# Score products over pairs of chunks, keys turned without a stride, and value products per pair of kv heads in a hybrid decoder step

## The chip, the cores and the metric

The kernel runs on one core of one Trainium2 chip as one launch. The metric is the device time of that launch in microseconds (us), as the median of several runs. A profiled execution of the same program gives the rows used below: for each engine what ran when, and what ended its waits. The engines are TensorE (PE, and PEld for its weight loads), VectorE (DVE), ScalarE (ACT), GpSimd (POOL) and SyncE (SP), which issues most of the transfers.

## The reference, cut to what matters

The program is one step of a two-layer decoder: 512 prompt tokens and, for each of 8 requests, 8 new tokens behind 2048 cached ones. Layer 0 mixes by pooling, layer 1 is sparse attention; each is followed by a gated FFN. The change touches only the attention of the new tokens in layer 1. There each of 16 heads (4 query heads for each of 4 kv heads, 64 wide) attends in three branches: to compressed rows, to 16 selected blocks of 64 rows, and to a window of 512 rows. The three results are weighed by gates and added.

```python
N_HEADS = 16
KV_HEADS = 4
HEAD_DIM = D_MODEL // N_HEADS
Q_PER_KV = N_HEADS // KV_HEADS
SEL_BLOCK = 64
N_SEL = 16
WINDOW = 512

def masked_softmax(s, mask):
    s = jnp.where(mask, s.astype(jnp.float32), NEG)
    return jnp.where(mask, jax.nn.softmax(s, axis=-1), 0.0)
```

All of it is float32. The selected branch is computed over all 2048 cached rows, with a bias of -1e30 on the rows of blocks that aren't selected.

## The kernel before

`sample_attention` (L1055) holds the attention of the new tokens. For each request `b` there are five **chunks** `ch`: chunk 0 is the window of 512 rows, chunks 1 to 4 are 512 rows each of the selected-branch cache. That makes 40 steps, `i = 5b + ch`. The 32 query rows of a kv head's group (4 heads by 8 tokens) and the 4 kv heads fill 128 partitions in the scores.

- `load(i)` (L1179) brings a raw tile of 512 rows, four rows to a partition (row `4p + j`), keys in the first 256 columns of each row and values in the other 256. The window comes by SP's DMA (L1189), and its rows go out again to an output (L1191); the other four chunks come by a gather that POOL issues (L814). There are 12 raw slots; the values of a chunk free its slot.
- `prepare(i)` (L1197) turns the keys on DVE by 32 by 32 squares (L1205) into `kf`, of which there are two buffers. The transpose writes every fourth word, so that the keys stand in the cache's own order (`n j`).
- `score(i)` (L1217) makes 32 products (2 halves of the head's 64 columns, 4 row groups `q`, 4 kv heads `g`), each on a 32 by 32 tile of PE, of 128 columns (L1236), into one of four places of a ring in PSUM. DVE adds the bias, takes the maximum and writes `sc` (L1244). `softmax` follows after chunk 0 and after chunk 4 (L1251, ACT's exponentials L1260, L1261).
- `turn` (L1266) brings a chunk's weights into rows by four transposes on PE (tile `ppt`, L202) and a copy on ACT (`ph`, L1275).
- `values` (L1279) multiplies them with the chunk's values: 4 rows `j` by 4 kv heads, 16 products of 64 columns on tiles of 128 rows by 32 columns (L1294), into `po`. Its sixth call for a request takes the compressed rows (`cvb`) and the new tokens (`VT`). `outputs` (L1297) and `outputs2` (L1309) add the branches and turn the result.

A float32 product is two records on PE, and two weight loads on PEld. At step `i` the loop (L1317) calls `load(i+5)`, `prepare(i+1)`, `score(i)`, and `turn` and `values` of the request before. A scheduler orders each engine's queue by what each instruction needs, so that the program's order is a wish and not a rule. Ahead of the loop stands the compression of cached rows for all 8 requests (`rounds` L942, with DVE's transposes `xf` at L882, the splits `xlo` at L886, the hidden rows `hs`, `hgh`, `hgl` at L932 to L939, and the compressed values `cvf`, which go by DMA to `cvd`, L988 to L990). The first keys of the attention are turned during its last rounds. Other places that rows name are `select` (L1153) and `select2` (L1171), which choose blocks, `qq` (L1094), the queries by 32 by 32 squares, and L1430, a product of the prompt's attention.

Of the kernel before, what the change touches and what calls it, by code (L numbers as in the profile page):

```python
# [9 lines left out]
F32 = mybir.dt.float32  # L10
# [11 lines left out]
NB = 8  # L22
# [33 lines left out]
PT = 4  # L56
SR = 5
WORD = (0, 1, 2, 3, 4)

# [69 lines left out]
def body(tc, top, I, O):  # L129
# [925 lines left out]
    def sample_attention(ctx):  # L1055
# [4 lines left out]

        VT = sa.tile([128, 4, 2, 64], F32, name="VT")

# [13 lines left out]
        with ExitStack() as c1:  # L1076
# [6 lines left out]
            for j in range(2):  # L1083
                c0 = KC + 512 * (j + 1) + 256
                sp.dma_start(VT[64 * j:64 * j + 64, :, j], pjd[:, c0:c0 + 256].rearrange("t (g c) -> t g c", g=4))

# [27 lines left out]

        kp_ = Slots(ctx, "sk", kf=2)
        more = Slots(ctx, "sv")
# [78 lines left out]
        kv, prepared = {}, set()  # L1195

        def prepare(i):  # L1197
            if i >= len(steps) or i in prepared:
                return
            b, ch = steps[i]  # L1200
            prepared.add(i)
            raw = raws.pop(i)

            kf = kp_.tile([128, 2, 4, 128], F32, tag="kf", name=f"kf{b}{ch}")
            dve.transpose(kf.rearrange("p f g (n j) -> p j g f n", j=4), raw[:, :, 0:256].rearrange("p j (g f i) -> p j g f i", g=4, f=2))  # L1205
            kv[b, ch] = (kf, raw)

        def attend(between):
# [6 lines left out]
            ring = mmt("pss", "s", 4)  # L1215

            def score(i):  # L1217
                b, ch = steps[i]
                kf, _ = kv[b, ch]
                if i % 5 == 0:  # L1220
# [10 lines left out]
                pt = ring[:, :, (i % 4) * 128:(i % 4 + 1) * 128]  # L1231
                for f in range(2):
                    for q in range(4):
                        for g in range(4):
                            qs = slice(32 * q, 32 * q + 32)
                            pe.matmul(pt[32 * g:32 * g + 32, q], qq[qs, b, g, f], kf[qs, f, g], start=f == 0, stop=f == 1,  # L1236
                                      tile_position=(32 * q, 32 * g))
                by_key = "p (q n j) -> p q n j"
# [40 lines left out]
            def values(b, ch):  # L1279
                ph = pend.pop((b, ch))  # L1280
                cvb = st[b][4]
                if ch == 0:
                    po[b] = mmt(f"po{b}")
                raw = kv.pop((b, ch))[1] if ch < 5 else None
                for j in range(4 if ch < 5 else 2):
                    for g in range(4):
                        if ch < 5:
                            v, c0 = raw[:, j, 256 + 64 * g:320 + 64 * g], 64 if ch == 0 else 0
                        elif j == 0:
                            v, c0 = cvb[:, 64 * g:64 * g + 64], 128  # L1290
                        else:
                            v, c0 = VT[:, g].rearrange("q s c -> q (s c)"), 0
                        rs = slice(32 * g, 32 * g + 32)
                        pe.matmul(po[b][rs, c0:c0 + v.shape[1]], ph[:, j, rs], v,  # L1294
                                  start=ch == 0 and j == 0, stop=ch == 5 and j == 1, tile_position=(0, 32 * g))

            def outputs(b):  # L1297
                osb = scp.tile([128, 3, 64], F32, tag="osb", name=f"osb{b}")
                mx = st[b][2]
                tmp = osb[:, 2]  # L1300
                act.activation(tmp, po[b][:, 128:192], AF.Copy)
                dve.scalar_tensor_tensor(tmp, po[b][:, 64:128], mx[:, 15:16], tmp, OP.mult, OP.add)

                twice = [128, 2, 64]
                dve.scalar_tensor_tensor(osb[:, 0:2], po[b][:, 0:64].unsqueeze(1).broadcast_to(twice), mx[:, 11:12],
                                         tmp.unsqueeze(1).broadcast_to(twice), OP.mult, OP.add)
                return osb[:, 0:2].rearrange("p s c -> p (s c)")

# [7 lines left out]

            prepare(0)  # L1317
            for i in range(len(steps) + 7):
                b, ch = divmod(i, 5)
                between(i)  # L1320
                load(i + SR)
                prepare(i + 1)
                if b < NB:
                    score(i)
                    if ch == 3:
                        turn(b, 0)
                if 0 < b <= NB:
                    if ch >= 1:
                        turn(b - 1, ch)
                    if ch == 4:  # L1330
                        turn(b - 1, 5)
                    if ch >= 2:
                        values(b - 1, ch - 1)
                if b < NB and ch == 4:
                    values(b, 0)
                if b > 1:
                    if ch == 0:
                        values(b - 2, 4)
                        values(b - 2, 5)
                        pend["o"] = outputs(b - 2)  # L1340
                    elif ch == 1:
                        outputs2(b - 2, pend.pop("o"))
# [466 lines left out]
```

## Time and profile before

| quantity | value |
|---|---|
| median of 3 runs | 1721.8 us (1721.6 to 1725.24) |
| the profiled execution: time | 1727.31 us |
| its span in the trace | 1725.5 us |
| PE, PEld busy in the span | 1625.2 us, 1504.4 us |
| DVE, ACT, POOL busy | 1044.1, 758.7, 405.0 us |
| new tokens' scores, first to last product | 854.3 to 1022.8 us of the span |
| bytes moved by DMA | 206.35 MB |

The profiled execution took 5.5 us more than the median, and 1.8 us of its time lie around the span. The page cuts the span in 40 slices and gives for each the busy share of the engines in tenths. Of these slices, numbers 21 to 24 (863 to 1035 us) show PE at 7 to 8 tenths, DVE at 5 to 7, and the clock granted to PE at 6 to 7 tenths. In most other slices PE stands at 9. The rows behind these words, and those of the waits, follow in a section of their own.

### The profile page before, as it was taken

The numbers are of one execution on the slowest core, as the hardware profiler recorded it, in microseconds if no ns is written. First come the engines' busy times: TensorE is split into PE (matmuls) and PEld (weight loads), VectorE is DVE, ScalarE is ACT, GpSimd is POOL, SyncE is SP. The second block draws the span as 40 slices with busy tenths as digits, with TensorE's granted clock in tenths as the row PEclk, the third lists the DMA queues.
The fourth block names the chain that finished last, engine by engine and source line by source line (L and its number), as shares of the span: only waits on it lengthen the run. The fifth ranks groups of instructions, "written<-read, shape, count | busy, mean of one in ns | idle before, by whom it ended". The sixth has DMA issues, their size and how long they took to land.

```text
span 1725.5 us, 36745 instructions
## 1 busy us (share of the span) xinstructions
PE 1625.2 (94%) x15447; PEld 1504.4 (87%) x15447; DVE 1044.1 (61%) x2029; ACT 758.7 (44%) x1384; POOL 405.0 (23%) x602
## 2 busy tenths in 40 slices
PE   8999999999999999999877788999999999999995
PEld 7999999999999999999754454555999999999995
DVE  7666454545574448888775556767366555464547
ACT  5654334343353325566533235656155535344331
POOL 2222111111020023433311204665022112011104
PEclk9999999999999999999967778999999999999998
DMA  5232232223257746645657771001412232222311
GB/s 188 82 99 99 66 106 75 80 68 98 63 183 244 191 149 217 227 150 183 226 200 275 241 218 43 1 1 45 135 50 74 74 98 74 74 98 74 98 59 55
DMA packets 123461, 206.35 MB, mean 120 GB/s; under 512 B 19039, under 2 KB 98745, under 8 KB 112832
## 3 DMA queue, kind: packets, MB, share of 16 engines
q1 hardware_dynamic: 113392, 134.49, 24.7%
q0 software_dynamic: 9216, 67.11, 11.4%
q8 instruction: 121, 1.98, 0.5%
q10 hardware_dynamic: 688, 2.40, 0.4%
q14 instruction: 44, 0.36, 0.1%
HBM read 178.85 MB, written 24.84 MB: 118 GB/s over the span
## 4 chain that ended last, share of the span: by engine, by line
PE 79%; issue 7%; DVE 7%; POOL 4%; ACT 3%; DMA 1%; SPq 0%; ACTq 0%; POOLq 0%; DVEq 0%
PE u L165 31%; PE d L165 14%; PE pr L911 10%; PE pj L165 7%; PE pss L1236 3%; PE wo L165 2%; POOL P L1505 2%; PE ppt L202 2%; PE psp L1486 1%; PE po L1294 1%; PE pop L1534 1%; PE pj L709 1%; DVE kf L1205 1%; DVE wla L257 1%; DVE lnst L320 1%
## 5 line engine op out<-in xcount | busy, mean ns | idle before, releaser
L165 PE MATMUL u<-xl,wha 128*128 128x288 f32 x704 | 208.0, 296 | 0.3 <-POOL xl L351 0.2
L165 PE MATMUL u<-xl,whb 128*128 128x288 f32 x704 | 208.0, 296 | 0.2
L165 PE MATMUL u<-xh,whb 128*128 128x288 f32 x704 | 207.3, 295 | 0.0
L165 PE MATMUL u<-xh,wha 128*128 128x288 f32 x704 | 207.3, 295 | 0.0
L165 PE MATMUL u<-xh,wla 128*128 128x288 f32 x704 | 207.2, 295 | 0.0
L165 PE MATMUL u<-xh,wlb 128*128 128x288 f32 x704 | 207.2, 295 | 0.0
L417 POOL COPY fcol<-u 128x18 f32<-128x18 f32 x88 | 68.0, 782 | 467.8 <-ACT u L416 467.8
L422 DVE SCALAR_TENSOR_TENSOR c<-u,convp,c 128x592 f32<-128x592 f32 x88 | 72.3, 832 | 123.1 <-ACT c L421 123.1
L257 DVE TENSOR_TENSOR wla<-rawa,wha 128x2048 fp32r<-128x2048 f32 (+1 forms) x52 | 99.5, 1918 | 68.6 <-ACT wha L256 67.9
L257 DVE TENSOR_TENSOR wlb<-rawb,whb 128x2048 fp32r<-128x2048 f32 x37 | 84.8, 2293 | 86.4 <-ACT whb L256 86.4
L165 PEld LDWEIGHTS u<-xl,wha 128*128 128x128 f32 x704 | 132.0, 188 | 2.0 <-DVE xl L351 1.1
L165 PEld LDWEIGHTS u<-xl,whb 128*128 128x128 f32 x704 | 132.0, 188 | 1.9 <-DVE xl L351 1.1
L165 PEld LDWEIGHTS u<-xh,wha 128*128 128x128 f32 x704 | 132.0, 188 | 0.1
L165 PEld LDWEIGHTS u<-xh,whb 128*128 128x128 f32 x704 | 132.0, 188 | 0.1
L165 PEld LDWEIGHTS u<-xh,wlb 128*128 128x128 f32 x704 | 132.0, 188 | 0.0
L165 PEld LDWEIGHTS u<-xh,wla 128*128 128x128 f32 x704 | 132.0, 188 | 0.0
L503 DVE SCALAR_TENSOR_TENSOR xz<-xz,d 128x288 f32<-128x288 f32 x160 | 70.4, 451 | 87.7 <-PE d L165 87.2
L256 ACT ACTIVATE wha<-rawa 128x2048 fp32r<-128x2048 f32 (+1 forms) x52 | 83.1, 1617 | 91.1 <-PE d L165 58.9
L256 ACT ACTIVATE whb<-rawb 128x2048 fp32r<-128x2048 f32 x37 | 70.9, 1915 | 114.3 <-PE d L165 32.0
L911 PE MATMUL pr<-xlo,W1h 128*128 128x256 f32 x512 | 104.6, 286 | 2.7 <-DVE xlo L886 2.7
L911 PE MATMUL pr<-xhi,W1h 128*128 128x256 f32 x512 | 105.6, 288 | 0.0
L165 PE MATMUL d<-hh,wha 128*128 128x288 f32 x352 | 104.4, 298 | 0.1
(654 smaller groups left out, 4614.6 us busy)
## 6 DMA issues: line engine op xcount, KB each, us to landing
rawa<-in_ffn_w_up SPq DMA_DIRECT2D x22, 1024.0 KB
rawb<-in_ffn_w_up SPq DMA_DIRECT2D x22, 1024.0 KB
rawa<-in_ffn_w_down SPq DMA_DIRECT2D x11, 1024.0 KB
rawb<-in_ffn_w_down SPq DMA_DIRECT2D x11, 1024.0 KB
rawa<-in_nsa_w_in SPq DMA_DIRECT2D x9, 1024.0 KB
sr<-in_state_win_kv SPq DMA_DIRECT2D x8, 1024.0 KB
out_win_kv_s<-sr SPq DMA_DIRECT2D x8, 1008.0 KB
rawb<-in_nsa_w_o SPq DMA_DIRECT2D x16, 256.0 KB
```

The source lines that it names most:

```text
L165: pe.matmul(out, a, b, start=first and j == 0, stop=last and j == n - 1)
L202: pe.transpose(out, in_, ident[:in_.shape[0], :in_.shape[0]])
L256: act.activation(h[:, a:b], r[:, a:b], AF.Copy)
L257: dve.tensor_tensor(lo[:, a:b], r[:, a:b], f32(h[:, a:b]), OP.subtract)
L320: dve.bn_stats(self.st[:, t, q], pt[:LT])
L417: pool.tensor_copy(col[:, :, m].rearrange("p (j i) -> p j i", i=2), u[:, TP:TP + 90].rearrange("p (j i) -> p j i", i=10)[:, :, 0:2])
L422: dve.scalar_tensor_tensor(c, u[:, 1:1 + CW], cv[:, 44 + m:45 + m], c, OP.mult, OP.add)
L503: dve.scalar_tensor_tensor(z, z, ALPHA if first else 1.0, p_[:, :HALF], OP.mult, OP.add)
L709: pe.matmul(*args, start=k == 0 and i == 0, stop=k == KD - 1 and i == 1)
L911: pe.matmul(banks[b, kv][ri][:, :, gh * nn:(gh + 1) * nn], W1[wi][:, kv, ri * 8 + th * 4 + c], xx[:, c // 2, c % 2].rearrange("p g n -> p ...
L1236: pe.matmul(pt[32 * g:32 * g + 32, q], qq[qs, b, g, f], kf[qs, f, g], start=f == 0, stop=f == 1, tile_position=(32 * q, 32 * g))
L1505: pool.tensor_tensor(x, x, st[:, 2, e, t:t + 1].broadcast_to([128, (t + 1) * 128]), OP.mult)
```

## The change

Three things change, all of them in `sample_attention`.

1. **Scores by groups of chunks.** The five chunks of a request form three groups: chunk 0 alone, 1 with 2, 3 with 4. A group has one `kf`, and `products` makes its 32 products at once, of 128 columns or, for a pair, of 256. DVE's transpose now writes its words side by side, so the keys stand in the order `j n`. The order of the cache is restored where PE writes into PSUM: there each product's words are written four words apart (a view `s j n` of a place laid out as `s n j`). There are three `kf` buffers, each of up to two chunks, where there were two of one chunk.
2. **Keys earlier.** Three chunks are prepared ahead of the loop, and step `i` prepares `i + 3`, where it was one and `i + 1`.
3. **Values by pairs of kv heads.** Each value product takes the weights of two kv heads (a tile of 128 rows by 64 columns) and the values of both, 128 columns; half of what it computes, one head's weights with the other's values, is not used. A chunk has 8 products of 128 columns instead of 16 of 64. `VT`, `po` and `outputs` follow: `po` has 384 columns where 192 were, and `outputs` takes a copy of 128 columns on ACT and two steps of 128 columns on DVE.

The records of the products fall from 2560 to 1536 for the scores, and from 1408 to 704 for the values; each record has its weight load.

```diff
-        VT = sa.tile([128, 4, 2, 64], F32, name="VT")
+        VT = sa.tile([128, 2, 2, 128], F32, name="VT")
...
-        kp_ = Slots(ctx, "sk", kf=2)
+        kp_ = Slots(ctx, "sk", kf=KB_)
...
+        groups = [g for b in range(NB) for g in ([5 * b], [5 * b + 1, 5 * b + 2], [5 * b + 3, 5 * b + 4])]
+        group_of = {i: n for n, g in enumerate(groups) for i in g}
...
-            kf = kp_.tile([128, 2, 4, 128], F32, tag="kf", name=f"kf{b}{ch}")
-            dve.transpose(kf.rearrange("p f g (n j) -> p j g f n", j=4), raw[:, :, 0:256].rearrange("p j (g f i) -> p j g f i", g=4, f=2))
-            kv[b, ch] = (kf, raw)
+            n = group_of[i]
+            g = groups[n]
+            if i == g[0]:
+                kv["k", n] = kp_.tile([128, 2, 4, len(g), 128], F32, tag="kf", name=f"kf{n}")
+
+            at = order_of(g).index(i)
+            dve.transpose(kv["k", n][:, :, :, at].rearrange("p f g (j n) -> p j g f n", j=4),
+                          raw[:, :, 0:256].rearrange("p j (g f i) -> p j g f i", g=4, f=2))
+            kv[b, ch] = raw
+
+        def order_of(g):
+            return sorted(g, key=lambda i: i % 4)
...
+            def products(n):
+                g = order_of(groups[n])
+                b = steps[g[0]][0]
+                kf = kv.pop(("k", n))
+                places = ring.rearrange("p q (s n j) -> p q s j n", s=4, j=4)[:, :, g[0] % 4:g[-1] % 4 + 1:max(1, g[-1] % 4 - g[0] % 4)]
+                for f in range(2):
+                    for q in range(4):
+                        for h in range(4):
+                            qs = slice(32 * q, 32 * q + 32)
+                            pe.matmul(places[32 * h:32 * h + 32, q], qq[qs, b, h, f], kf[qs, f, h].rearrange("p s (j n) -> p s j n", j=4),
+                                      start=f == 0, stop=f == 1, tile_position=(32 * q, 32 * h))
+
             def score(i):
                 b, ch = steps[i]
-                kf, _ = kv[b, ch]
+                if i == groups[group_of[i]][0]:
+                    products(group_of[i])
...
-                for f in range(2):
-                    for q in range(4):
-                        for g in range(4):
-                            qs = slice(32 * q, 32 * q + 32)
-                            pe.matmul(pt[32 * g:32 * g + 32, q], qq[qs, b, g, f], kf[qs, f, g], start=f == 0, stop=f == 1,
-                                      tile_position=(32 * q, 32 * g))
...
-                    for g in range(4):
+                    for p in range(2):
                         if ch < 5:
-                            v, c0 = raw[:, j, 256 + 64 * g:320 + 64 * g], 64 if ch == 0 else 0
+                            v, c0 = raw[:, j, 256 + 128 * p:384 + 128 * p], 128 if ch == 0 else 0
...
-                        rs = slice(32 * g, 32 * g + 32)
-                        pe.matmul(po[b][rs, c0:c0 + v.shape[1]], ph[:, j, rs], v,
-                                  start=ch == 0 and j == 0, stop=ch == 5 and j == 1, tile_position=(0, 32 * g))
+                        pe.matmul(po[b][64 * p:64 * p + 64, c0:c0 + v.shape[1]], ph[:, j, 64 * p:64 * p + 64], v,
+                                  start=ch == 0 and j == 0, stop=ch == 5 and j == 1)
...
-            prepare(0)
+            for i in range(3):
+                prepare(i)
...
-                prepare(i + 1)
+                prepare(i + 3)
```

The lines of the kernel after have other numbers: the scores' products are L1239 there (L1236 before), the transposes of the keys L1214 (L1205), `sc` L1264 (L1244), the value products L1313 (L1294), and a line of the compression is one higher.

Two places show how the order of the work moves. The first is DVE at the end of the compression. Before, one chunk's transpose (`kf`) stands there ahead of the last rounds; the names `xf`, `xlo`, `hs` and `hgl` are the compression's.

```order
L1205 STREAM_TRANSPOSE kf_10192<-sr_9924 128x4x4x2x32
L886 TENSOR_TENSOR xlo_9976<-xf_9974,xhi_9975 128x1024
L882 STREAM_TRANSPOSE xf_10074<-crp 128x2x4x2x32
L1134 TENSOR_REDUCE cm_9967<-psc_9964 128x1
L1135 TENSOR_TENSOR stl<-psc_9964,cst 128x16
L882 STREAM_TRANSPOSE xf_10093<-crp 128x2x4x2x32
...
L932 TENSOR_TENSOR hs_10111<-pr_9838,hs_10111 128x4x127
L886 TENSOR_TENSOR xlo_10095<-xf_10093,xhi_10094 128x512
L939 TENSOR_TENSOR hgl_10116<-hs_10111,hgh_10115 128x512
```

The same place of DVE's queue after:

```order
L1214 STREAM_TRANSPOSE kf_10195<-sr_9927 128x4x4x2x32
L1214 STREAM_TRANSPOSE kf_10195<-sr_9929 128x4x4x2x32
L887 TENSOR_TENSOR xlo_9979<-xf_9977,xhi_9978 128x1024
L1135 TENSOR_REDUCE cm_9970<-psc_9967 128x1
L1136 TENSOR_TENSOR stl<-psc_9967,cst 128x16
L883 STREAM_TRANSPOSE xf_10077<-crp 128x2x4x2x32
L1214 STREAM_TRANSPOSE kf_10303<-sr_9931 128x4x4x2x32
L883 STREAM_TRANSPOSE xf_10096<-crp 128x2x4x2x32
...
L887 TENSOR_TENSOR xlo_10098<-xf_10096,xhi_10097 128x512
L1214 STREAM_TRANSPOSE kf_10303<-sr_9933 128x4x4x2x32
L940 TENSOR_TENSOR hgl_10119<-hs_10114,hgh_10118 128x512
```

The transposes of chunks 2, 3 and 4, which stood among the attention's own steps, now stand among the last rounds of the compression, that of chunk 4 just ahead of the last `hgl`.

The second place is PE's queue in the middle of the attention, from a request's last value products on. Before:

```order
L1294 MATMUL po_11890<-VT,ph_12217 32x128 x4
L1236 MATMUL pss<-kf_12255,qq 32x128 x32
L202 MATMUL ppt_12370<-cst,sc_11912 128x128 x4
L202 MATMUL pot_12377<-cst,osb_12329 128x128
L202 MATMUL ppt_12418<-cst,sc_11912 128x128 x3
L1236 MATMUL pss<-kf_12335,qq 32x128 x32
L202 MATMUL ppt_12418<-cst,sc_11912 128x128
L1294 MATMUL po_12235<-sr_11643,ph_12375 32x64 x16
L202 MATMUL ppt_12478<-cst,sc_12257 128x128
L1236 MATMUL pss<-kf_12383,qq 32x128 x32
```

And after, from such a place on:

```order
L1313 MATMUL po_11402<-VT,ph_11627 64x256 x2
L1239 MATMUL pss<-kf_11549,qq 32x2x4x32 x32
L203 MATMUL ppt_11751<-cst,sc_11448 128x128 x4
L203 MATMUL pot_11758<-cst,osb_11711 128x128
L203 MATMUL ppt_11767<-cst,sc_11448 128x128 x4
L1313 MATMUL po_11637<-sr_11245,ph_11756 64x128 x8
L1239 MATMUL pss<-kf_11649,qq 32x2x4x32 x32
L203 MATMUL ppt_11819<-cst,sc_11683 128x128 x4
```

A pair's 32 products stand where two groups of 32 stood, and 8 value products where 16 stood; the turns (`ppt`) between them are the same. On DVE two evictions (`sc`) follow each other and then two transposes, three or four chunks ahead.

## Rows read from the trace of the kernel before

**Rows 1.** Busy time of engines by stretch: the attention's start and middle.

```profile
core 0: us, PE busy (x) PEld busy (x) DVE busy (x) ACT busy (x) POOL busy (x), PEclk, DMA share, GB/s
854.00:884.00 30.00, 23.66 (x766) 16.88 (x766) 26.29 (x56) 10.16 (x20) 3.57 (x5) 0.69 0.40 140
884.00:1010.00 126.00, 92.96 (x2779) 64.81 (x2783) 78.15 (x149) 38.92 (x87) 22.99 (x31) 0.74 0.75 265
```

**Rows 2.** Who waited for whom, 884 to 1010 us: total us, times, longest.

```profile
DVE sc L1244 <- PE pss L1236: 31.4, 20, 3.1
PE pss L1236 <- issue: 25.1, 17, 3.5
...
PE po L1294 <- issue: 2.0, 2, 1.6
```

**Rows 3.** Chain that ended last, 854 to 884, then 884 to 1010 us.

```profile
by line: DVE kf L1205 26.6%; PE pss L1236 25.9%; DVE sc L1244 14.4%; issue 9.3%; PE po L1294 5.3%; PE ppt L202 3.1%; ACT sc L1260 2.7%; DVE blk L1153 2.2%; PE psb L1171 1.9%; DVE hidp L932 1.0%; ACT ptl L1261 1.0%; DVE mx L1263 0.8%; DVE bl
...
by line: PE pss L1236 31.8%; issue 25.3%; PE ppt L202 18.4%; PE po L1294 17.4%; DVE kf L1205 3.2%; DVE sc L1244 1.5%; ACT ptl L1261 0.7%; PE pot L202 0.7%; ACT sc L1260 0.5%; DVE mx L1262 0.4%; DVE mx L1244 0.1%; DVE mx L1263 0.1%; DVE mx L
```

**Rows 4.** DMA, 884 to 1010 us: packets, MB, share; median us to landing.

```profile
DMA packets 5183, 33.41 MB, mean 265 GB/s; under 512 B 567, under 2 KB 1207, under 8 KB 1207
...
q8 instruction: 22, 0.36, 1.1%
...
sr<-in_cache_slc_kv,idx POOLq DMA_INDIRECT x20, 8.5
```

**Rows 5.** The page: PE's instructions and its instruction queue, whole span.

```profile
PE 1625.2 (94%) x15447; PEld 1504.4 (87%) x15447; DVE 1044.1 (61%) x2029; ACT 758.7 (44%) x1384; POOL 405.0 (23%) x602
...
q8 instruction: 121, 1.98, 0.5%
```

**Rows 6.** All score products: ns min/median/max, first and last start, form.

```profile
L1236 PE MATMUL pss<-kf,qq x2560: 264/412/419, 854.3 to 1022.8; 32*32 32x128 f32 x197
```

**Rows 7.** Timeline of PE: one chunk's products, one chunk's values, twice.

```profile
864.15 1.52 PE L1236 MATMUL pss<-kf,qq 32*32 32x128 f32 x64 [1.58 <-DVE mx L1244]
865.61 1.08 PE L1294 MATMUL po<-sr,ph 128*32 128x64 f32 x32
...
876.44 1.07 PE L1236 MATMUL pss<-kf,qq 32*32 32x128 f32 x64 [0.50 <-DVE mx L1244]
877.43 0.65 PE L1294 MATMUL po<-sr,ph 128*32 128x64 f32 x32
```

**Rows 8.** Stretches as in rows 1: the granted clock at those moments.

```profile
863.00:866.60 3.60, 2.45 (x96) 1.79 (x96) 3.57 (x10) 0.21 (x1) 0.00 (x0) 0.50 0.02 5
876.40:878.00 1.60, 1.56 (x96) 1.20 (x96) 1.60 (x2) 0.17 (x1) 0.00 (x0) 1.00 0.04 10
```

**Rows 9.** Products of 512 columns on four tiles; eight in the chain.

```profile
L1430 PE MATMUL pk<-Q,KB x32: 592/617/1063, 1044.1 to 1148.6; 128*32 128x512 f32 x32
...
1107.07 1.00 PE pk L1430 x8
```

**Rows 10.** VectorE's transposes: chunk keys, compressed rows, queries.

```profile
L1205 DVE STREAM_TRANSPOSE kf<-sr x40: 1985/2036/2141, 821.2 to 1017.2; 128x1024 f32<-128x1024 f32 x40
...
L882 DVE STREAM_TRANSPOSE xf<-cr x128: 661/696/712, 597.1 to 826.6; 128x512 f32<-128x512 f32 x128
...
L1094 DVE STREAM_TRANSPOSE qq<-q x1: 2268/2268/2268, 682.5 to 682.5; 128x2048 f32<-128x2048 f32 x1
```

**Rows 11.** Timeline ahead of the attention: two gathers, one VectorE piece.

```profile
826.95 0.95 POOL L814 DMA_INDIRECT sr<-in_cache_slc_kv,idx  x1 [4.55 <-DVE xf L882]
...
839.19 1.47 POOL L814 DMA_INDIRECT sr<-in_cache_slc_kv,idx  x1 [3.64 <-DVE xf L882]
...
844.16 1.43 DVE L939 TENSOR_TENSOR hgl<-hs,hgh 128x512 fp32r<-128x512 f32 x1 [1.15 <-ACT hgh L938]
```

**Rows 12.** Chain into the attention's first product.

```profile
847.95 4.39 DMA cvd<-cvf
...
854.27 1.54 PE pss L1236 x63
```

More of the change, by code (lines that the diff above doesn't have):

```diff
@@ L57 @@
 SR = 5
+KB_ = 3
 WORD = (0, 1, 2, 3, 4)
@@ L1084, in sample_attention @@
                 c0 = KC + 512 * (j + 1) + 256
-                sp.dma_start(VT[64 * j:64 * j + 64, :, j], pjd[:, c0:c0 + 256].rearrange("t (g c) -> t g c", g=4))
+                sp.dma_start(VT[64 * j:64 * j + 64, :, j], pjd[:, c0:c0 + 256].rearrange("t (a c) -> t a c", a=2))
             q4 = s1.tile([128, NB, 4, 64], F32, name="q4")
@@ L1283, in values @@
                     po[b] = mmt(f"po{b}")
-                raw = kv.pop((b, ch))[1] if ch < 5 else None
+                raw = kv.pop((b, ch)) if ch < 5 else None
                 for j in range(4 if ch < 5 else 2):
-                    for g in range(4):
+                    for p in range(2):
                         if ch < 5:
-                            v, c0 = raw[:, j, 256 + 64 * g:320 + 64 * g], 64 if ch == 0 else 0
+                            v, c0 = raw[:, j, 256 + 128 * p:384 + 128 * p], 128 if ch == 0 else 0
                         elif j == 0:
-                            v, c0 = cvb[:, 64 * g:64 * g + 64], 128
+                            v, c0 = cvb[:, 128 * p:128 * p + 128], 256
                         else:
-                            v, c0 = VT[:, g].rearrange("q s c -> q (s c)"), 0
-                        rs = slice(32 * g, 32 * g + 32)
-                        pe.matmul(po[b][rs, c0:c0 + v.shape[1]], ph[:, j, rs], v,
-                                  start=ch == 0 and j == 0, stop=ch == 5 and j == 1, tile_position=(0, 32 * g))
+                            v, c0 = VT[:, p].rearrange("q s c -> q (s c)"), 0
+                        pe.matmul(po[b][64 * p:64 * p + 64, c0:c0 + v.shape[1]], ph[:, j, 64 * p:64 * p + 64], v,
+                                  start=ch == 0 and j == 0, stop=ch == 5 and j == 1)
             def outputs(b):
-                osb = scp.tile([128, 3, 64], F32, tag="osb", name=f"osb{b}")
+                osb = scp.tile([128, 128], F32, tag="osb", name=f"osb{b}")
                 mx = st[b][2]
[L1300 to L1307, printed above, removed]
+                act.activation(osb, po[b][:, 256:384], AF.Copy)
+                for j in (1, 0):
+                    dve.scalar_tensor_tensor(osb, po[b][:, 128 * j:128 * j + 128], mx[:, 11 + 4 * j:12 + 4 * j], osb, OP.mult, OP.add)
+                return osb
             def outputs2(b, osb):
```

## Prediction

> **What bounds the kernel now.** I read the busy time by stretch first, since the change lies in the new tokens' attention alone, and its stretches differ. At the start, 854 to 884 us, DVE is busy 26.29 of 30 us; in the middle, 884 to 1010 us, PE is busy 92.96 of 126 us, DVE 78.15 and the DMA engines 0.75 of the time [rows 1]. Then who waits for whom: in the middle DVE waits 31.4 us for score products, so PE is ahead of it in the chain, while PE's own idle time stands mostly at "issue", 25.1 us before scores in 17 places and 2.0 us before values in 2 [rows 2]. The chain that ended last says the same: at the start DVE's key transposes hold 26.6% of it and its evictions 14.4%; in the middle scores hold 31.8%, issue 25.3%, turns 18.4%, values 17.4%, and the key transposes 3.2% [rows 3].
>
> What is "issue"? PE waits for no engine there. In the same 126 us its instruction queue q8 moved 22 packets [rows 4]; over the whole span there are 121 for 15447 products and 15447 loads [rows 5], which is 30894/121 = 255 instructions a packet, and 22 x 255 = 5610 is about the 2779 + 2783 that PE and PEld ran there [rows 1]. I read the idle time as waiting for the instructions themselves: (25.1 + 2.0)/22 = 1.23 us a packet.
>
> **The change part by part.** The sum is made against the profiled execution's 1727.3 us, which lies 5.5 us above the median.
>
> *A, fewer instructions.* 1024 score records and 704 value records go, each with its load: 3456 instructions or 13.5 packets. At 1.23 us that is **-16.7 us**. The other bound is 0, if what delays PE is a refill that comes as often for other reasons.
> The Trainium skill ("Runtime: NRT & Kernel Launch", section "Instruction fetch mechanics") says that the sequencer fetches ahead and that crossing a block is mostly hidden. By that, A would be near 0 and the sum 16.7 us higher. The trace disagrees in this stretch, as 27.1 us of PE's idle time have no other releaser [rows 2].
>
> *B, scores.* A chunk's 64 records took 1.52 us at one moment and 1.07 at another, a chunk's 32 value records 1.08 and 0.65 [rows 7]; the granted clock was 0.50 and 1.00 then [rows 8], that is 1.2 and 2.4 GHz. The middle's mean of 0.74 [rows 1] is 48% of the time at the upper level and 52% at the lower, so a chunk's scores cost 0.48 x 1.07 + 0.52 x 1.52 = 1.30 us, a request's five 6.50. After, a request has one single group and two pairs, each of 64 records. A pair's tiles take 2 products x 2 records x 256 = 1024 columns each; as many on each of four tiles took 1.00 us at the upper level [rows 9]. The lower bound is that records, not columns, set the pace: 1.07. I add the start and end of the sixteen tiles, 1.2 at the upper level and 1.95 at the lower, mean 1.59. So 1.30 + 2 x 1.59 = 4.48, 2.0 less a request, **-16 us** for eight. The lower bound gives 6.50 - 3.90 = 2.6 a request, -21.
>
> *C, values.* Before 0.48 x 0.65 + 0.52 x 1.08 = 0.87 us a chunk. After, each of two tiles takes 4 products x 2 records x 128 = 1024 columns, 1.00 us by [rows 9], and at the lower level between 1.00 x 1.08/0.65 = 1.66 and 2.00: I take 1.75, mean 1.39. That is +0.52 for each of 40 chunks, +21. The sixth call goes from 384 columns a tile to 768, +0.37 at the upper level, +0.4 at the mix, +3 for eight. Together **+24 us**. So the change trades columns for instructions: on columns alone it would lose.
>
> *D, DVE's transposes.* With the stride 1024 columns take 2036 ns; without, 512 take 696 and 2048 take 2268 [rows 10], so 1024 should take 1.22 us: 0.82 us or 40% less. On the chain the transposes hold 0.266 x 30 + 0.032 x 126 = 12 us [rows 3]; 40% of it is -5, and some evictions come sooner behind them: **-6 us**. The bounds are 0 (PE is late next) and -12 (all of it goes).
>
> *E, the start.* Transposes of chunks 2 to 4 move ahead of the last compression rounds. The one for chunk 4 stands before the last `hgl`, which ran at 844.16; of the gathers before the attention one is issued at 826.95 and one at 839.19, 1.47 us long [rows 11], and in this kernel a gather lands 8.5 us after issue (median of the middle) [rows 4]. If chunk 4's gather is issued after the transposes that free POOL, at about 843, its landing at 851 to 852 holds `hgl`, and behind it wait `cvf`, the 4.39 us of its DMA and the first scores at 854.27 [rows 12]: +8 us. But then the keys of five chunks are ready, and the start is the stretch that DVE bounds; five transposes were 5 x 2.04 = 10 us of its 30. I take **0**, between -3 and +8.
>
> *F.* `outputs` has steps of 128 columns where it had 64 and 128, eight times, beside DVE time that waits for PE [rows 2]: 0; without that cover some 0.1 us each. The third key buffer and its size delay some early gathers; that is in E and G.
>
> *G, transposes three ahead.* DVE now asks for chunk i+3 at step i. A slot comes free some six steps before its chunk's turn; steps are (1022.8 - 854.3)/39 = 4.3 us apart [rows 6], so a gather has three steps, about 12 us, against a median of 8.5 [rows 4]. Behind a transpose that waits stand the next evictions, and PE's next group behind these. Late gathers I price at **+2.5 us**; bounds 0 and +8.
>
> Sum: -16.7 - 16 + 24 - 6 + 0 + 2.5 = -12, or 1715 us for the profiled execution and **1709 us** on the median.
>
> **The rivals.**
>
> *R1, strided writes into PSUM slow the score products (slower).* The change takes the stride from DVE and gives it to PE, which writes each product's words four apart. No row shows a product that does so. For: the same stride costs DVE a factor of 2.036/1.22 = 1.67 [rows 10]. Against: single score products are not at their column rate (512 columns a tile in 1.07 us, where 1024 take 1.00 [rows 7, 9]), so some cost hides. With 1.67 a pair's columns take 1.67 and 2.77 us, mean 2.24: 0.65 x 16 = +10, 1720 us. If the second half of the head (which adds to what stands there) reads with the stride as well, I take 2.5: pairs 3.36, +28, singles +3, so 1740 us. It decides where a pair takes more than 2.6 us on average: there the gain and 0.2% are used up.
> The Trainium skill speaks against the change here: "PSUM — Partial Sum Buffer", section "Specifications (TRN2)", has lines of 8 bytes and says that any non-contiguous pattern slows matmuls significantly. It names no factor, and no run here shows it.
>
> *R2, the fetches stay.* If the waits at issue keep half or all of their time though fewer instructions run, the sum is 8 to 17 us higher: 1718 to 1726. For: a packet is fetched while DMA is at 0.75 [rows 1], and a denser kernel may make each fetch slower. Against: stalls and packets agree in number.
>
> *R3, gathers hold DVE.* The 8 us of E are not regained and G comes to 5: 1719 to 1723. For: DVE's queue is in order, and transposes now stand ahead of evictions that were free to go. Against: keys are ready for five chunks.
>
> *R4, the clock.* With the upper level kept all through, a request's scores take 1.07 + 2.4 = 3.5 us instead of 4.5 and its values 5.0 instead of 7.0: -24 us for eight; half of that is likely at most, so 1697 and down to 1686. For: longer products leave PE fewer gaps. Against: the mean was 0.69 and 0.74 in the two stretches [rows 1]. Its mirror, more time at the lower level, gives about 1720.
>
> **How the numbers follow.** 0.2% (3.4 us) is about what a measurement of this kernel can tell from no change, so "same" is 1718.4 to 1725.2. The forecast, 1700 to 1718, has 0.50, of which 0.47 falls on faster and 0.03 on same. R4 has 0.11 (faster), its mirror 0.05 (same). R1 has 0.06 (same, factor 1.67) and 0.14 (slower, 2.5). R2 has 0.04 same and 0.02 slower, R3 0.05 and 0.03. Together 0.58 faster, 0.23 same, 0.19 slower. The range from 1690 to 1736 leaves out the lower part of R4 (about 0.04) and the upper part of R1 (about 0.12); the forecast's own range is 1700 to 1718.
>
> **What would show it.** Right: the same stretch of the attention with about 13 q8 packets and some 16 us of issue instead of 22 and 27; transposes of 1.2 us; a pair's 64 records in 1.2 us at the upper clock; a chunk's 16 value records in 1.0; steps of about 4.0 us. Wrong: pairs above 2.6 us at the mix (R1); issue time unchanged at fewer packets (R2); DVE's waits for `sr` transfers, and a first product after 862 us with chunk 7 no sooner than before (R3); a granted clock far from 0.74 (R4).

## The result and the profile after

The kernel after takes 1701.19 us (median of 4 runs, 1700.27 to 1701.98) against 1722.87 us for the kernel before: a ratio of 0.9872, with a 95% interval from 0.9855 to 0.989. That is 22 us less. On a second chip the same two kernels stood at 1698.23 and 1714.88 us, a ratio of 0.9905 (0.9873 to 0.9937), 17 us less. The forecast was 12 us less (1709 us), and its range of 1700 to 1718 just holds the 1701.19 us.

First the busy time by stretch of the kernel after; its first two lines answer to [rows 1]. The columns are the same: us, busy time (and count) of PE, PEld, DVE, ACT and POOL, granted clock, DMA share, GB/s.

```profile
854.00:884.00 30.00, 23.10 (x478) 15.37 (x478) 20.53 (x64) 11.15 (x23) 4.22 (x7) 0.72 0.51 190
884.00:1010.00 126.00, 102.59 (x1904) 74.20 (x1903) 64.23 (x171) 47.23 (x107) 23.54 (x33) 0.86 0.78 281
```

The stretches are equal in time and not in work: after the change the same 126 us hold more of it. PE runs a third fewer records in the middle and is busy longer; the granted clock there is 0.86 where it was 0.74. Who waited for whom, from 884 to 1010 us of the kernel after (engine, line, what it waited for: us in total, times, longest), answers to [rows 2]:

```profile
DVE kf L1214 <- DMA sr<-in_cache_slc_kv,idx: 21.8, 13, 2.8
PE pot L203 <- DVE mx L1283: 18.9, 5, 4.3
...
DVE kf L1214 <- DMA sr<-in_state_win_kv: 13.0, 5, 3.1
...
DVE sc L1264 <- PE pss L1239: 4.8, 5, 1.8
...
PE pss L1239 <- issue: 1.5, 5, 0.3
```

This is another kernel to read. PE's waits at "issue", 27.1 us before (28.5 with one of 1.4 us before a turn, which [rows 2] leaves out), are down to 1.5. DVE hardly waits for products any more (31.4 us before, 4.8 now). Instead DVE waits 34.8 us for loads, which it did not do in [rows 2], and PE waits 18.9 us for DVE ahead of one small product, the turn of the outputs (`pot`). The DMA view of the same stretch, as in [rows 4], and the products and transposes by line, as in [rows 6] and [rows 10] (duration min/median/max in ns, first and last start):

```profile
q8 instruction: 15, 0.25, 0.7%
...
sr<-in_cache_slc_kv,idx POOLq DMA_INDIRECT x21, 7.1
...
L1239 PE MATMUL pss<-kf,qq x1536: 263/382/632, 858.0 to 999.1; 32*32 32x256 f32 x128, 32*32 32x128 f32 x64
...
L1214 DVE STREAM_TRANSPOSE kf<-sr x40: 1202/1245/1246, 818.3 to 993.6; 128x1024 f32<-128x1024 f32 x40
```

Why does PE wait five times for DVE? The chain that ended last shows one request of the middle (start, us, what; pieces of under 0.1 us are left out):

```profile
906.41 8.77 DMA sr<-in_state_win_kv
915.20 1.25 DVE kf L1214
916.45 0.23 DVE osb L1321
916.75 0.32 DVE osb L1321
917.21 0.45 PE pot L203
917.66 0.85 PE ppt L203 x4
918.51 1.91 PE po L1313 x16
920.42 2.48 PE pss L1239 x64
922.89 1.16 PE ppt L203 x8
924.06 1.02 PE po L1313 x16
925.08 0.90 PE ppt L203 x6
925.98 1.05 PE po L1313 x16
927.04 8.46 DMA sr<-in_state_win_kv
```

Read it as a ring. A window's load starts when values free its slot, and takes 8.8 us. The transpose of its keys waits at the head of DVE's queue for it. Behind that transpose stand the outputs of an earlier request, behind these on PE's queue `pot`, then turns, then values, which free the slot of the next window. From 906.41 to 927.04 is 20.6 us, and the next loads start at 947.5 and 968.3: every request takes that long, whatever PE could do. Before the change a request of the middle took 24.6 us, from one window's eviction to the next (mean from the third to the seventh).

This is the chain of one execution. In the profile on the second chip the same kernel has the same pace (20.7 us a request) and the same wait of PE (17.7 us ahead of `pot`), but the chain that ended last goes another way:

```profile
925.77 13.75 DMA sr<-in_cache_slc_kv,idx
...
939.54 2.37 DVE kf L1214 x2
...
941.92 0.69 DVE sc L1264
...
945.49 0.94 POOL sr L815
...
947.43 13.47 DMA sr<-in_cache_slc_kv,idx
```

A gather lands late, two transposes wait for it, two evictions stand behind them, and behind these POOL, which fills a bias buffer that the evictions read, issues the next gathers. DVE waits 31.6 us for gathers there and 4.7 for windows. Both profiles show loads and the transposes that wait for them as the pace; which load closes the ring differs between them.

### The profile page after: what moved, and what is told of

Read it like the earlier page. It is cut to its first block, busy times and chain, and to the rows that moved or that the text cites. A ratio compares the mean times of both kernels' runs of the same rounds, so it can differ in the third digit from the quotient of the medians.

```text
span 1698.8 us, 33275 instructions
## 1 busy us (share of the span) xinstructions
PE 1609.8 (95%) x13719; PEld 1496.5 (88%) x13719; DVE 1014.4 (60%) x2029; ACT 756.8 (45%) x1384; POOL 408.0 (24%) x602
## 4 chain that ended last, share of the span: by engine, by line
PE 72%; DVE 8%; issue 6%; DMA 5%; POOL 4%; ACT 3%; SPq 0%; ACTq 0%; POOLq 0%; DVEq 0%
PE u L166 32%; PE d L166 13%; PE pj L166 7%; PE pr L912 7%; PE wo L166 3%; DMA sr<-in_state_win_kv 3%; POOL P L1521 2%; PE po L1313 2%; DMA sr<-in_cache_slc_kv,idx 1%; PE pop L1550 1%; PE ppt L203 1%; PE psp L1502 1%; PE pss L1239 1%; PE pj L710 1%; DVE wla L258 1%
## 5 line engine op out<-in xcount | busy, mean ns | idle before, releaser
L912 PE MATMUL pr<-xhi,W1h 128*128 128x256 f32 x512 | 104.8, 286 | 0.0
```

The lines of the kernel that those rows point to most:

```text
L912: pe.matmul(banks[b, kv][ri][:, :, gh * nn:(gh + 1) * nn], W1[wi][:, kv, ri * 8 + th * 4 + c], xx[:, c // 2, c % 2].rearrange("p g n -> p ...
```

## The experiments

Each was timed beside the kernel before on its own chip. The first four ran on one chip, where before took 1714.46 us, the next four on that of the second comparison above, the last four on a third, so ratios are compared rather than times.

**Values alone.** The kernel before with the value products, `VT` and `outputs` of the change:

```diff
-                    for g in range(4):
+                    for p in range(2):
...
-                        pe.matmul(po[b][rs, c0:c0 + v.shape[1]], ph[:, j, rs], v,
+                        pe.matmul(po[b][64 * p:64 * p + 64, c0:c0 + v.shape[1]], ph[:, j, 64 * p:64 * p + 64], v,
```

> The kernel before with the value products by pairs of kv heads alone (scores, keys and their order as before). 704 records fewer, more columns. Theory 1, a fixed price for each instruction packet (1.23 us): -6.8 us for 5.5 packets, +24 for the columns, so about 1740 us, and 1.1 to 1.3 us of issue time a packet in the middle of the attention. Theory 2, a race (PE waits only where it runs through a packet's instructions faster than the next one arrives): longer value products use up the time that was waited, so issue time falls from 27 to under 12 us in a stretch of the same work and the time stays within 1718 to 1730 us.

1704.43 against 1714.46 us, ratio 0.9935 (0.9909 to 0.9961). A part that by a fixed price a packet loses 17 us gains 10. The time also lies below the 1718 to 1730 us that the race theory gave. Its middle, 884 to 1010 us:

```profile
884.00:1010.00 126.00, 104.93 (x2637) 79.25 (x2635) 90.10 (x169) 44.69 (x101) 23.39 (x33) 0.86 0.82 284
...
PE pss L1236 <- issue: 4.0, 4, 1.6
...
q8 instruction: 21, 0.34, 1.1%
```

21 packets came in this stretch, one less than before, but PE waited 4.0 us and not 27. The theory of a fixed price is out; the race stands. The clock rose to 0.86 with this part alone, which neither theory had; how much of the 10 us is the clock's isn't separated.

**Scores and keys alone.** The kernel after with the values of before (the diff above, the other way round).

> The kernel after with the value products, VT, po and outputs of before (16 products of 64 columns a chunk); pairs of chunks, unstrided keys and three chunks ahead stay. Theory 1: 5.5 packets more than after at 1.23 us, 24 us of columns less: 1684 us if PE alone sets the pace. Theory 2: fetch waits of 5 to 15 us come back in place of the columns: about 1692 to 1700. Theory 3 (the loop of a window slot: values free it, its load lands 9 us later, the transpose that waits for it holds DVE and with it PE, 20.6 us a request): shorter values shorten that loop by at most 2 us a request, so 1690 to 1700, with PE waiting for DVE before the transpose of outputs as in after.

1700.92 us, ratio 0.9921 (0.9897 to 0.9945), just above what the race and the ring gave. Waits at issue stay in part, 14.6 us in the three lines, and the clock stays low:

```profile
884.00:1010.00 126.00, 92.98 (x2475) 62.28 (x2463) 64.42 (x171) 46.79 (x107) 23.10 (x32) 0.73 0.78 281
...
PE pss L1239 <- issue: 10.3, 8, 2.4
...
PE ppt L203 <- issue: 2.7, 1, 2.7
...
PE po L1314 <- issue: 1.6, 1, 1.6
```

The two parts alone gain 0.65% and 0.79%, together 0.95% on the second chip and 1.3% on the first. With intervals of 0.2 to 0.3% each, these numbers don't show whether the parts add up. The waits at issue can't: of 28.5 us, values alone leave 4.0 and scores alone 14.6, so each takes away some that the other takes too.

**Two chunks ahead.** The kernel after with

```diff
-            for i in range(3):
+            for i in range(2):
                 prepare(i)
...
-                prepare(i + 3)
+                prepare(i + 2)
```

> The kernel after with keys prepared two chunks ahead instead of three (two ahead of the loop, prepare(i+2)). Theory 3 (the window's transpose waits three chunks ahead for a load whose slot has just come free, and holds the evictions and outputs behind it): DVE's waits for window loads fall from 13.0 us to under 5, PE's wait for DVE before the outputs' transpose (18.9 us) goes, and the time falls by 6 to 15 us to 1686 to 1695. Rival, the DMA engines' throughput is the bound (0.78 of the time busy): the waits move elsewhere and the time stays within 1697 to 1705.

1696.93 us, ratio 0.9898 (0.9876 to 0.9919): no different from the kernel after within the intervals, and not the 1686 to 1695 us that were expected. The waits hardly changed:

```profile
PE pot L203 <- DVE mx L1283: 18.3, 5, 4.5
...
DVE kf L1214 <- DMA sr<-in_state_win_kv: 10.5, 4, 3.1
```

In the two traces DVE runs its transposes, evictions and outputs in the same order. The scheduler moves a transpose forward as soon as it has a key buffer, so the call's place in the program did not matter, and this run repeats the kernel after rather than testing the theory. The number of key buffers does change the order, which a later kernel tries.

**The stride back on DVE.** Keys are written every fourth word as before, products write PSUM side by side; pairs and the rest stay.

```diff
-            dve.transpose(kv["k", n][:, :, :, at].rearrange("p f g (j n) -> p j g f n", j=4),
+            dve.transpose(kv["k", n][:, :, :, at].rearrange("p f g (n j) -> p j g f n", j=4),
...
-                places = ring.rearrange("p q (s n j) -> p q s j n", s=4, j=4)[:, :, g[0] % 4:g[-1] % 4 + 1:max(1, g[-1] % 4 - g[0] % 4)]
+                places = ring.rearrange("p q (s k) -> p q s k", s=4)[:, :, g[0] % 4:g[-1] % 4 + 1:max(1, g[-1] % 4 - g[0] % 4)]
...
-                            pe.matmul(places[32 * h:32 * h + 32, q], qq[qs, b, h, f], kf[qs, f, h].rearrange("p s (j n) -> p s j n", j=4),
+                            pe.matmul(places[32 * h:32 * h + 32, q], qq[qs, b, h, f], kf[qs, f, h],
```

> The kernel after with the stride given back to the transpose: keys are written every fourth word on DVE as before, and the score products write PSUM side by side; pairs of chunks, three ahead and values by pairs of kv heads stay. If strided writes slow the products, a pair's 64 records fall from 1.49 us at the upper clock level to 1.1 to 1.2; if not, they stay at 1.4 to 1.5. Transposes go back from 1.245 to 2.04 us. Time: 1695 to 1700 if the products' stride costs more than DVE's; 1702 to 1710 if DVE's stride costs more, since DVE holds PE at the outputs.

1711.04 us, ratio 0.9981 (0.9961 to 1.0001): nearly all of the gain is gone. The timeline of PE shows a pair at either clock level, first with the stride on PE (the kernel after), then without (this kernel):

```profile
865.99 1.49 PE L1239 MATMUL pss<-kf,qq 32*32 32x256 f32 x64
...
873.40 2.38 PE L1239 MATMUL pss<-kf,qq 32*32 32x256 f32 x64
```

```profile
867.07 1.49 PE L1239 MATMUL pss<-kf,qq 32*32 32x256 f32 x64 [1.28 <-DVE mx L1264]
...
876.77 2.38 PE L1239 MATMUL pss<-kf,qq 32*32 32x256 f32 x64
```

1.49 and 2.38 us both ways. The stride costs PE nothing that these rows show, and DVE 0.8 us a chunk. On the time it is worth 0.9981 less 0.9905 or 0.76%, some 13 us, with intervals that leave 6 to 20. The larger part of what the traces show of it lies at the start of the attention and not in the ring:

```profile
854.00:884.00 30.00, 19.63 (x440) 13.18 (x448) 25.19 (x62) 11.32 (x23) 4.75 (x9) 0.72 0.42 158
```

DVE is busy 25.19 us here, 20.53 in the kernel after. From the first score product to the third window's eviction it takes 35.9 us (31.3 and 30.7 in the two profiles of after), from there to the last window's 106.3 (103.2 and 104.8).

**No loads.** In the kernels before and after, steps 12 to 39 keep the rows that lie in their slots:

```diff
+            if i >= SR + VN:
+                raws[i] = kept[n]
+                return
...
-            raws[i] = raw
+            raws[i] = kept[n] = raw
```

> The kernel before, with the row loads, gathers and window copies of chunk steps 12 to 39 left out: those steps work on the rows that lie in their slots, so outputs of the new tokens are of other rows. PE's instructions are the same. Theory 1, a fixed price a packet: 22 packets still cost about 27 us of issue time in the middle, and the time falls by under 8 us. Theory 2, a race between PE and packets that come through the same DMA engines as the rows: without that traffic issue time falls under 8 us in the middle, and the time falls by 15 to 30 us.

> The kernel after, with the same loads, gathers and copies of steps 12 to 39 left out. Theory 3 (loads and the transposes that wait for them now set the pace): the 20.6 us a request of the middle fall to PE's own work, 102.59/126 x 20.6 = 17 us or less, so 15 to 25 us off the time. Rival (PE sets the pace and the waits are slack): under 5 us off.

The kernel after ran beside them unchanged:

> The kernel after, unchanged, beside the kernels of this group on one chip. Its ratio to the kernel before should be within 0.984 to 0.990. If the wait for instructions is a race with transfers, the kernel before, which has it, should scatter more from run to run than this one, which hardly has it: over 8 us between lowest and highest before, under 5 us here. With a fixed price a packet both scatter alike.

Before without loads: 1690.35 us (ratio 0.9862). After without loads: 1656.66 us (0.9665), 42 us below the kernel after, where 15 to 25 were expected. Of the first, 884 to 1000 us, busy time, PE's idle time and packets:

```profile
884.00:1000.00 116.00, 96.03 (x3135) 68.63 (x3139) 85.31 (x169) 45.27 (x104) 3.76 (x11) 0.74 0.15 34
...
PE pss L1239 <- issue: 1.7, 4, 0.5
...
q8 instruction: 25, 0.41, 1.4%
```

PE ran the instructions of before, with 25 packets in 116 us, and waited 1.7 us for them. So the wait is no price of a packet but of a packet that arrives late beside the rows' traffic. The trace has the start of each q8 packet as well. From 884 to 970 us of the kernel before, 14 waits of over 0.7 us end 2.2 to 2.5 us after a packet has started, and the next packet starts 2.8 to 4.6 us after the wait's end. Without loads there are three waits of about 0.5 us and a shorter one; those three end 2.4 to 2.8 us after a packet's start, and the next packet starts 1.1 to 1.2 us later. The packets themselves take 0.9 and 1.0 us (medians). So PE does wait for packets, and it is their start that comes later beside the rows, not their transfer that takes longer; what holds the start back, no row shows. The clock stayed at 0.74: these waits are not what held it down. Of the second kernel the stretch from 884 to 960 us:

```profile
884.00:960.00 76.00, 75.10 (x1761) 57.88 (x1758) 61.22 (x162) 39.89 (x97) 3.47 (x9) 1.00 0.07 19
```

PE is busy 75.1 of 76 us, at the upper level all the time. In the kernel after PE is busy 58.65 us in this stretch, at a granted clock of 0.84. So the 42 us hold a higher clock as well, and the copies of the windows' rows, which are left out too. The scatter, which the unchanged kernel was to show, proves nothing: 5.3 us between lowest and highest of 4 runs, where under 5 was expected, and 11.3 us for 13 runs of before, but the kernel with the stride on DVE scatters by 9.4 us in 10 runs and has no waits at issue in its list.

**Window rows copied elsewhere.** Two chunks ahead, and the copies of the window's rows to their output read the input and not the raw tile:

```diff
-                sp.dma_start(O["win_kv_s"][0, b, 0:WIN - TS].rearrange("(p j) k g c -> p (j k g c)", j=4),
-                             raw[2:128].rearrange("p j c -> p (j c)"))
...
             fn["attend"](between)
+            for b in range(NB):
+                sp.dma_start(O["win_kv_s"][0, b, 0:WIN - TS].rearrange("(p j) k g c -> p (j k g c)", j=4),
+                             I["state_win_kv"][0, b, TS:WIN].rearrange("(p j) k g c -> p (j k g c)", j=4))
```

> The kernel after with keys two chunks ahead, as in the earlier run, and with the window's rows copied to their output straight from the input, not from the raw tile, by transfers that no longer stand in the attention (the scheduler puts them at the start of the program). If competition for the DMA engines makes window loads and gathers late, window loads land in 6 to 8 us instead of 9.3, a request takes 17 to 19 us in the middle instead of 20.6, and the time is 5 to 15 us below the run with two chunks ahead. If the loads' own latency does, no more than 3 us below; copies at the start may cost up to 3 us there.

1721.5 us, ratio 1.0035 (1.0015 to 1.0056): a little slower than before, far from either forecast. The loss lies at the other end of the program, where the copies now stand: from 150 to 600 us PE is busy 429.72 us where it was 448.34 with the copies in their old place, and the attention begins 26 us later. What waits for what there stays open. In the attention the window loads on the chain take 8.2 to 10.1 us and not 6 to 8, and the window's first and last evictions lie 126.9 us apart, against 128.7 with two chunks ahead alone. A share of 0.64 of the DMA engines' time instead of 0.80 thus does little: neither their throughput nor the copy is what makes a request take 20.6 us.

**Key buffers and slots.** Three kernels, all two chunks ahead: two key buffers instead of three (`KB_ = 2`), 14 raw slots instead of 12 (`VN = 9`), and both.

```diff
-VN = 7
+VN = 9
...
-KB_ = 3
+KB_ = 2
```

> The kernel after with two key buffers instead of three and keys two chunks ahead. With two buffers the scheduler can put the window's transpose only behind the outputs and a pair of evictions, since its buffer is still in use. Theory 3a, the transpose that waits for the window's load holds DVE ahead of the outputs: PE's wait for DVE before the outputs' transpose falls from 18 us in five places to under 6 us, a request takes 17 to 19 us in the middle instead of 20.6, and the time is 8 to 18 us below the run with three buffers and two chunks ahead. Theory 3b, the slots come free too late whatever DVE's order: the wait moves to the next transposes and the time stays within 4 us of that run.

> The kernel after with 14 raw slots instead of 12 and keys two chunks ahead, three key buffers as in after. Each load may start two chunks, some 8 us, sooner. Theory 3b: DVE's waits for loads (32 us in the middle) fall under 12 us, a request takes 15 to 18 us, and the time is 12 to 25 us below the run with 12 slots and two chunks ahead. Theory 3a: about 5 us below, since the window's transpose still stands ahead of the outputs. If the DMA engines' throughput is the bound: no change.

> Both edits: two key buffers, 14 raw slots, keys two chunks ahead. If both theories hold, the fastest of the three, 1672 to 1685 us by the times of after; if slots alone matter, as the run with 14 slots; if DVE's order alone, as the run with two buffers.

Two buffers: 1684.84 us, ratio 0.983 (0.9779 to 0.9881). 14 slots: 1674.66 us, 0.9762 (0.9714 to 0.9811). Both: 1671.12 us, 0.9754 (0.9704 to 0.9804), the fastest of all that do the whole work; between the last two the intervals don't decide. Waits from 884 to 970 us, first in the kernel after, then with two buffers, with 14 slots, and with both edits:

```profile
DVE kf L1214 <- DMA sr<-in_cache_slc_kv,idx: 17.3, 10, 2.8
...
PE pot L203 <- DVE mx L1283: 15.9, 4, 4.3
```

```profile
DVE kf L1214 <- DMA sr<-in_cache_slc_kv,idx: 12.0, 6, 3.7
...
PE pot L203 <- DVE mx L1283: 6.4, 4, 2.8
```

```profile
DVE kf L1214 <- DMA sr<-in_cache_slc_kv,idx: 19.2, 12, 3.4
...
DVE kf L1214 <- DMA sr<-in_state_win_kv: 0.9, 1, 0.9
```

```profile
PE pss L1239 <- issue: 4.0, 4, 1.7
...
DVE kf L1214 <- DMA sr<-in_cache_slc_kv,idx: 1.8, 2, 1.1
PE pot L203 <- DVE mx L1283: 1.8, 3, 0.6
```

With two buffers the window's transpose stands behind the outputs and a pair of evictions, and PE's wait for DVE ahead of `pot` falls from 15.9 to 6.4 us. With 14 slots that wait is gone from the list, and DVE hardly waits for windows (11.0 us in the kernel after). Its waits for gathers stay at 19.2 us, where under 12 were expected for all loads, so this part of theory 3b failed. A request of the middle takes 20.3 us with two chunks ahead alone, 17.5 with two buffers, 16.9 with 14 slots and 15.2 with both. So both links of the ring are real: a transpose that stands ahead of the outputs, and a slot that comes free late. Taking away either shortens it. With both gone the transfers may be the next limit, which no run tests:

```profile
884.00:970.00 86.00, 77.08 (x1772) 57.13 (x1769) 60.93 (x161) 40.00 (x93) 22.01 (x29) 1.00 0.94 372
```

The DMA engines are now busy 0.94 of the time and move 372 GB/s, where after had 0.80 and 306 in the same stretch, while PE has the upper level throughout.

**14 slots without the change.** The kernel before with `VN = 9` alone.

> The kernel before with 14 raw slots instead of 12, nothing else. If loads set the pace only since the change (before, PE and its waits for instructions did), the time stays within 6 us of the kernel before and its issue time in the middle stays above 15 us. If loads were late in the kernel before as well, it gains 12 us or more, and part of what 14 slots gave after the change was there to be had before it.

1719.99 us against 1713.14, ratio 1.0051 (1.0024 to 1.0077): a little slower, by 7 us where within 6 was expected. Its middle still waits for instructions:

```profile
PE pss L1236 <- issue: 20.2, 12, 4.3
```

Slots are worth nothing before the change and, by 0.9762 against 0.9898 (two chips), some 23 us after it. The bound moved.

## Why the prediction was right, and where it was not

The direction held, and the terms that made the gain were named. That the time fell into the range is in part luck: A and G had the wrong mechanism, B and C the wrong size, and a higher clock was no term of the sum. A and the clock gave more than forecast, B, C and G less, and these misses nearly cancelled.

*A, fewer instructions.* The step that failed is the price: 1.23 us for each packet. 27.1 us of idle time became 1.5 with 15 packets instead of 22; by the price 18 us would have been left. The wait is the outcome of a race: how long PE takes for the instructions it has, against how long the next packet takes beside the rows' traffic. Values alone left 21 packets and 4.0 us; no loads left 25 packets and 1.7 us. So R2, by which half or all of the waits would stay, did not come, and A was worth about 26 us in this stretch rather than 16.7, and the extra columns of C were in good part paid out of the same waits, as the gain of values alone suggests. An average over stalls was taken for a cost of each. The rule that I weighed against it ("Runtime: NRT & Kernel Launch", section "Instruction fetch mechanics", of the Trainium skill, fetches are mostly hidden) holds in the run without loads (1.7 us) and in the kernel after (1.5 us); it does not hold in the kernel before, with its short products beside 265 GB/s of row traffic (27.1 us).

*B, scores.* A pair took 1.49 and 2.38 us at the two levels where I had 1.2 and 1.95. At the mix of before this is 1.95 a pair, so 1.3 us less a request instead of 2.0: 10 us, not 16. The reason is not the stride (R1): pairs take the same without it. What makes a pair slower than 1024 columns on four tiles stays open. The rule for R1 ("PSUM — Partial Sum Buffer", section "Specifications (TRN2)", of the Trainium skill) shows no effect on these products (1.49 and 2.38 us with the stride and without), and the measurement decides.

*C, values.* In the timeline of PE 16 records took 1.09 us at the upper level (I had 1.00) and 1.98 at the lower (1.75). At the mix of before that is 1.55 us a chunk and not 1.39, so +27 us for 40 chunks instead of +21. What the term left out is that the clock rose with it.

*D, transposes.* 1.245 us, as forecast (1.22). The term was sized by their share of the old chain, -6; giving the stride back in the new kernel costs some 13 us, the larger part at the start, where the prediction had two thirds of it too.

*E, the start.* The first product is 3.7 us later (858.0), and by the third request's window this is regained: its eviction starts at 889.3 us, 890.5 before. Right.

*G, loads.* Priced at 2.5 us, bounds 0 and 8. In the middle alone DVE waited 34.8 us for loads and PE 18.9 behind it. The step that failed is the comparison of three steps' time with the median landing of the old kernel: a window's load starts only when values free its slot, these wait for PE, PE for outputs, and they for DVE, which waits for the load. The rival for it (R3) had the mechanism, in a small size and with gathers; the ring is closed by the window's load in one profile and by gathers in the other. Without loads the kernel is 42 us faster, so this is where most of the possible gain stayed.

*R4, the clock.* It went the way of R4 in part: 0.86 for 0.74 in the middle. Values by pairs did it: every kernel with them has 0.81 or more there, and the four with value products on tiles of 32 columns have 0.73 to 0.75, whether PE waits 27.1 us at issue or 1.7. Which property of these products the clock follows was not tried.

One part of the difference between the two profiled executions isn't the change's. The prompt's attention takes 159.0 us from its first `pk` to its last `P` in the profile of before and 151.8 after; in the profile of before without loads it takes 151.7. So 7 of the 26.7 us between the spans aren't the change's: the granted clock was 0.92 there, against 0.97 in the kernel after. Whether other executions of before have it too isn't known. The attention itself ends 19.4 us sooner. The medians, 22 and 17 us apart, are the better measure.

## What to carry to other kernels

When "issue" idles TensorE, count packets, but don't price them: ask how long the engine works on a packet's instructions and what else moves through the DMA engines at that moment; fewer, longer instructions took nearly all of such a wait away here. When a change shortens the engine that bounds a loop, follow one buffer slot round, from the last reader to the load, to the first reader in its queue, and see what stands behind that reader: here two more slots and one key buffer less gave about as much again as the change itself. A transform that can be done by any of several engines' access patterns belongs where its stride is free.

## What the runs showed of the hardware that was not expected

- A float32 product's write to PSUM with words four apart took as long as one side by side: 1.49 and 2.38 us at the two clock levels for 64 records of 256 columns on 32 by 32 tiles, both ways.
- The wait for instructions depended on other traffic: 27.1 us in 126 at a DMA share of 0.75, 1.7 us in 116 at 0.15, with the same instructions.
- The granted clock differed with the form of the value products, 0.86 on tiles of 64 columns and 0.74 on tiles of 32, though those with 64 do twice the columns.
